# Turning queries one step and keys three steps sooner inside the next half head's projections (differential attention, one core)

## The chip, the cores and the metric

The kernel runs on one core of a Trainium2 chip. The metric is the device time of one execution in microseconds; smaller is better. TensorE (PE in the profile, with its weight loads as PEld) does the matrix products, VectorE (DVE), ScalarE (ACT) and GpSimd (POOL) the element-wise work, and SyncE (SP) issues the DMAs.

## The reference

One decoder layer over 1024 tokens of width 1024: three branches (mLSTM, causal differential attention, cross-attention into a memory of 256 tokens) run on the same normalised input `h`, are gated, merged and projected, and an MLP follows. The change touches the differential attention, with 8 heads, each with two queries and two keys of width 64 and one value of width 128:

```python
def diff_attention(q, k, v, q_g, k_g, lam, subln_g, lam_init):
    q = rms_norm(q, q_g)
    k = rms_norm(k, k_g)
    ...
        s = jnp.einsum('bhcqd,bhckd->bhcqk', qblk, kt).astype(jnp.float32) * scale
        ...
        s = jnp.where(kpos[None, :] <= qpos[:, None], s, -jnp.inf)
        p = jax.nn.softmax(s, axis=-1)
        a = p[:, :, 0] - lam * p[:, :, 1]
        return jnp.einsum('bhqk,bhkv->bhqv', a.astype(vt.dtype), vt)
    ...
    o = rms_norm(o, subln_g) * (1.0 - lam_init)
```

## The kernel before, in words

**Numbers.** A float32 operand is kept as two parts, `hi` and `lo`: `split` (lines 107 to 115) has ScalarE cast the source to `hi` (L111, or L114 with a scale) and VectorE subtract it to get `lo` (L112, or L115). A product `mm3` (line 117) is three matmuls, hi·hi, hi·lo and lo·hi.

**Two streams woven into one.** `branch_d` runs a generator of projections, `d_gemm`, and between its steps issues the attention of the heads already projected. The projections go by half heads, j = 0 to 15: head j // 2, and tokens 0 to 511 (even j) or 512 to 1023 (odd j). A half head has four token tiles i of 128 tokens. A tile is eight steps k; a step is one `mm3`, that is three matmuls of 128x384 which add one slice of the contraction into a PSUM tile of the tag `mm`. So a half head has 32 steps, numbered i * 8 + k. After step 7 of a tile its result is read out of PSUM four times: a copy of query and key to `draw` (L947, ScalarE), their squares to `dscr` (L949, ScalarE), and the split of v into `dv` (L111 on ScalarE, then L112 on VectorE). The sums of squares go to `drr` (L953, VectorE) and, once for the four tiles, through POOL (L127, L128) to the reciprocal norms.

**Two PSUM banks take turns.** `mm_tile` hands out the tags `mm0` and `mm1` in turn, one bank each. While one tile is summed in one bank, the other bank holds the tile before it until that has been read.

**Turning.** The scores need queries and keys with the head's width along the partitions. `prep(raws, rr, vh)` returns three actions for the half head just projected, each with the step of the *next* half head behind which it is issued:

- `q_`: four transposes on TensorE (tile `pr`) of the queries of the four token tiles, put into the bank that is not being summed (`other_tile`, line 96); a split of the result into the tile `dsg` (L114, L115); four DMAs from `dsg` to `dq` (L882, SP's queue).
- `s_`: four multiplications on VectorE that scale the keys in `draw` by their norms (L887).
- `k_`: four transposes of the keys (again `pr`, in `other_tile`), a split into `dsg` (L111, L112), four DMAs from `dsg` to `dk` (L894, SP's queue).

There is one buffer of `dsg`, two of `dq` and four of `dk`. The turned tile stays in its bank until its split is done; the next token tile's projection starts in that same bank.

**The order on each engine.** With `pinned` set, `mm` and `transpose` keep TensorE's instructions in the order in which the program issues them (lines 86 to 94), and the four multiplications of `s_` are pinned among themselves and with these. The other instructions of VectorE, ScalarE, POOL and SP are ordered by a planner when the program is built, within their dependencies.

**Where the steps fall.** Ahead of the attention 60 steps of the projections are issued. Then, for each s (8 per head: a block of 128 queries), `branch_d` issues `scores(s, 0)`, three steps, `values(s-2)`, two steps, `scores(s, 1)`, one step, `turn(s-1, 0)`, one step, `turn(s-1, 1)`, one step and `combine(s)`; the norm of a finished half head is put in at three places. The very first s has seven steps and all others eight, so from then on the steps behind `scores(s, 0)` are k = 3, 4, 5 of a tile, those behind `values(s-2)` are 6 and 7, and 0, 1 and 2 follow around `turn`. `scores` writes two matmuls per 512 keys (tile `sc`), VectorE adds the mask and takes the maximum (L999), forms the exponential's bias (L1003), and ScalarE takes the exponential into `dpe` (L1007). `combine` forms the difference of the two softmaxes on VectorE (L1016, L1017, L1020), `turn` transposes it (tile `tp`) and splits it into `daT`, `values` multiplies it with `dv` (tile `po`, then L1058 on ScalarE and L1059 on VectorE into `doS`), and `norm` squares `doS` (L1068), sums it (L1070), takes the power on POOL (L127, L128), scales `doS` (L1074) and transposes and stores it (L1080, L327).

The last half head's three actions run within the steps of the gates that follow (`for n in range(NK * 4)`), with the same numbers.

Of the kernel before, what the change touches and what calls it, by code (L numbers as in the profile page):

```python
# [31 lines left out]
def f32(ap):  # L32
    return ap.bitcast(F32)
# [38 lines left out]
class Layer:  # L72
# [786 lines left out]
    def d_gemm(self, pool, kv, done):  # L859
# [5 lines left out]
        def prep(raws, rr, vh):  # L865

            qT = pool.tile([P, 2, 512], F32R, tag="dq", name=self.name("dq"))
            kk = pool.tile([P, 2, 2, 512], F32R, tag="dk", name=self.name("dk"))
            rows = [slice(0, 64), slice(64, 128)]

            def turned(j):
                pt = self.other_tile()
                for i in range(4):
                    self.transpose(pt[:, i * P : (i + 1) * P], raws[i][:, j * P : (j + 1) * P])
                return pt, pool.tile([P, 2, 512], F32R, tag="dsg", name=self.name("dsg"))

            def q_():
                pt, sg = turned(0)
                self.split(sg[:, 0], sg[:, 1], pt, self.gd)
                for c in range(2):  # L880
                    for h in range(2):
                        nc.sync.dma_start(f32(qT[rows[h], c]), f32(sg[rows[c], h]))  # L882

            def s_():
                for i in range(4):
                    k_ = raws[i][:, P : 2 * P].rearrange("p (c d) -> p c d", c=2)
                    self.pin(V.tensor_mul(k_, k_, rr[:, i, 2:4].unsqueeze(2).broadcast_to([P, 2, 64])))  # L887

            def k_():
                pt, sg = turned(1)  # L890
                self.split(sg[:, 0], sg[:, 1], pt)
                for c in range(2):
                    for h in range(2):
                        nc.sync.dma_start(f32(kk[rows[h], :, c]), f32(sg[rows[c]]))  # L894
                kv.append((qT, kk[:, 0], kk[:, 1], vh, rr))

            return [(4, q_), (5, s_), (13, k_)]

        raw = {}

# [14 lines left out]
        for j in range(16):  # L915
# [40 lines left out]
            rl = rr.rearrange("p a b -> p (a b)")  # L956
            self.rsqrt_mean(rl, rl, 64, 16)
            late = prep(raws, rr, vh)
            assert j < 4 or done[0] >= (j // 2 - 1) * 8
        for n in range(NK * 4):  # L960
# [810 lines left out]
```

## Time and profile before

| | |
|---|---|
| median of three runs | 2213.79 us (2211.71 to 2217.8) |
| the profiled execution's own time | 2213.57 us |
| its span, first to last instruction | 2211.8 us |
| mean granted clock of TensorE | 0.995 |
| VectorE busy | 1361.4 us (62%) |
| ScalarE busy | 980.7 us (44%) |
| POOL busy | 527.8 us (24%) |

Times within the trace count from the span's start. A timeline row gives start, duration, engine, line, operation, the tile written and the tiles read with their shapes, and the number of instructions merged into it; in brackets stands how long the engine was idle before it, and whose end released it. A row of waits gives the waiting instruction and the one waited for, the total in us, how often, and the longest. PE's ends are modelled and overlap the next start. Letters in tile names are the program's own, without buffer numbers.

### The profile page before, as it was taken

The numbers are of one execution on the slowest core, as the hardware profiler recorded it, in microseconds if no ns is written. First come the engines' busy times: TensorE is split into PE (matmuls) and PEld (weight loads), VectorE is DVE, ScalarE is ACT, GpSimd is POOL, SyncE is SP. The second block draws the span as 40 slices with busy tenths as digits, with TensorE's granted clock in tenths as the row PEclk, the third lists the DMA queues.
The fourth block names the chain that finished last, engine by engine and source line by source line (L and its number), as shares of the span: only waits on it lengthen the run. The fifth ranks groups of instructions, "written<-read, shape, count | busy, mean of one in ns | idle before, by whom it ended". The sixth has DMA issues, their size and how long they took to land.

```text
span 2211.8 us, 30588 instructions
## 1 busy us (share of the span) xinstructions
PE 2163.4 (98%) x11097; PEld 1860.7 (84%) x11097; DVE 1361.4 (62%) x2598; ACT 980.7 (44%) x1962; POOL 527.8 (24%) x696
## 2 busy tenths in 40 slices
PE   7999999999999999999999999999999999899999
PEld 5878888898899999999888888877787888688887
DVE  6643575565237777777641232544688877767779
ACT  6543355454336666666542120223444444543332
POOL 2100000000011111111000003202557655565553
PEclk9999999999999999999999999999999999999999
DMA  7023122121333333333343443436435444854444
GB/s 250 29 81 115 50 91 76 44 82 39 107 109 86 93 84 84 88 92 86 101 148 114 134 142 126 138 110 205 147 115 198 159 147 147 318 196 146 145 145 170
DMA packets 127948, 273.06 MB, mean 123 GB/s; under 512 B 12945, under 2 KB 21430, under 8 KB 125750
## 3 DMA queue, kind: packets, MB, share of 16 engines
q1 hardware_dynamic: 125494, 258.53, 37.2%
q10 hardware_dynamic: 2304, 12.58, 1.4%
q8 instruction: 87, 1.43, 0.3%
q14 instruction: 63, 0.52, 0.1%
HBM read 178.76 MB, written 67.14 MB: 111 GB/s over the span
## 4 chain that ended last, share of the span: by engine, by line
PE 77%; DVE 9%; DMA 6%; ACT 4%; issue 2%; POOL 2%; SPq 0%; DVEq 0%; ACTq 0%; POOLq 0%
PE mm L91 46%; PE p L91 20%; PE sc L91 6%; PE tp L94 2%; PE po L91 2%; DVE acc L67 1%; DMA kraw<-y 1%; DMA xr<-h_d 1%; DVE wo L67 1%; DMA y<-yd 1%; DVE u L67 1%; DVE w L112 1%; DMA wraw<-in_wup 0%; DVE xts L67 0%; DVE c L67 0%
## 5 line engine op out<-in xcount | busy, mean ns | idle before, releaser
L91 PE MATMUL mm<-w,hT 128*128 128x384 f32 (+3 forms) x2496 | 473.4, 332 | 8.3 <-DVE dsg L112 5.4
L91 PE MATMUL mm<-hT,w 128*128 128x512 f32 x1920 | 465.7, 395 | 0.0
L91 PEld LDWEIGHTS mm<-hT,w 128*128 128x128 f32 x1920 | 353.5, 188 | 74.2
L91 PEld LDWEIGHTS mm<-w,hT 128*128 128x128 f32 x2496 | 389.2, 190 | 22.2 <-DVE dsg L112 7.6
L91 PE MATMUL p<-xd,wo 128*128 128x512 f32 x1344 | 310.0, 393 | 5.7 <-DVE c L67 2.2
L91 PE MATMUL p<-xo,wo 128*128 128x512 f32 x1344 | 308.2, 390 | 5.7 <-DVE st L1418 2.6
L91 PEld LDWEIGHTS p<-xd,wo 128*128 128x128 f32 x1344 | 253.8, 189 | 61.7 <-DVE c L67 3.3
L91 PEld LDWEIGHTS p<-xo,wo 128*128 128x128 f32 x1344 | 251.0, 188 | 61.5 <-DVE u L67 3.7
L91 PE MATMUL mm<-kt,w 128*128 128x512 f32 x1152 | 262.2, 389 | 1.9 <-ACT w L111 1.1
L112 DVE TENSOR_TENSOR w<-raw,w 128x256 fp32r<-128x256 f32 (+3 forms) x304 | 173.0, 590 | 137.9 <-ACT w L111 136.8
L91 PEld LDWEIGHTS mm<-kt,w 128*128 128x128 f32 x1152 | 216.0, 188 | 47.9 <-ACT w L111 1.5
L111 ACT CAST w<-raw 128x256 fp32r<-128x256 f32 (+3 forms) x304 | 154.3, 530 | 178.9 <-PE mm L91 114.5
L104 ACT CAST wo<-wraw 128x896 fp32r<-128x896 f32 x122 | 115.0, 945 | 208.9 <-PE p L91 115.2
L67 DVE TENSOR_TENSOR wo<-wraw,wo 128x896 fp32r<-128x896 f32 x122 | 143.7, 1195 | 59.4 <-ACT wo L104 59.4
L1145 POOL TENSOR_TENSOR wraw<-wraw 128x128 f32<-128x128 f32 x128 | 97.3, 760 | 245.8 <-DMA wraw<-in_wdown 108.1
L1007 ACT ACTIVATE dpe<-sc,dst,drr 128x256 f32<-128x256 f32 (+7 forms) x128 | 106.7, 834 | 99.7 <-DVE dst L1003 92.0
L999 DVE CUSTOM_DVE_ANT_0 sc<-sc,tmask 128x256 f32<-128x256 f32 (+7 forms) x128 | 97.0, 758 | 12.6 <-PE sc L91 12.5
L127 POOL TENSOR_SCALAR hss<-hss 128x4 f32<-128x4 f32 x8 | 3.3, 410 | 415.4 <-ACT mscr L752 272.9
L91 PE MATMUL sc<-dk,dq 128*128 128x512 f32 (+3 forms) x384 | 90.4, 343 | 0.0
L1148 POOL TENSOR_TENSOR wraw<-wraw 128x128 f32<-128x128 f32 x128 | 85.6, 669 | 10.0
L1146 POOL TENSOR_TENSOR wraw<-wraw 128x128 f32<-128x128 f32 x128 | 87.3, 682 | 0.0
L1147 POOL TENSOR_TENSOR wraw<-wraw 128x128 f32<-128x128 f32 x128 | 87.2, 682 | 0.0
(283 smaller groups left out, 2832.6 us busy)
## 6 DMA issues: line engine op xcount, KB each, us to landing
dk<-dsg SPq DMA_DIRECT2D x64, 256.0 KB, 4.4
wraw<-in_wup SPq DMA_DIRECT2D x64, 256.0 KB, 3.4
r_d<-xts SPq DMA_DIRECT2D x16, 1024.0 KB, 4.1
wraw<-in_wdown SPq DMA_DIRECT2D x64, 256.0 KB, 3.1
xd<-r_d SPq DMA_DIRECT2D x19, 768.0 KB, 7.4
xd<-r_d SPq DMA_DIRECT2D x14, 1024.0 KB, 6.8
raw<-in_wgate SPq DMA_DIRECT2D x48, 256.0 KB, 3.2
gates<-gt SPq DMA_DIRECT2D x48, 256.0 KB, 2.0
```

The lines of the kernel that those rows point to most:

```text
L67: return self.tc.keep_in_program_order(f(*a, **k))
L91: self.pin(self.nc.tensor.matmul(out, l, r, start=start, stop=stop))
L94: self.pin(self.nc.tensor.transpose(out, x, self.ident))
L104: self.A.copy(hi, src)
L111: nc.scalar.copy(hi, src)
L112: nc.vector.tensor_sub(lo, src, f32(hi))
L999: V.tensor_tensor_reduce(out=sc[:, 0:n], in0=sc[:, 0:n], in1=self.tmask[:, D - n : D], scale=1.0, scalar=-3.0e38, op0=ALU.add, op1=ALU.max ...
L1007: nc.scalar.activation(pe[c][:, 0:n], sc[:, 0:n], AF.Exp, bias=t8[:, 2 + c : 3 + c], scale=rr[:, i, c : c + 1], accum_out=t8[:, 4 + c : 5 ...
L1145: G.tensor_add(r[:, 4], r[:, 0], r[:, 3])
L1146: G.tensor_sub(r[:, 5], r[:, 4], r[:, 1])
L1147: G.tensor_sub(r[:, 6], r[:, 1], r[:, 0])
L1148: G.tensor_sub(r[:, 7], r[:, 2], r[:, 5])
```

## The change

Only the two numbers that say behind which step of the next half head the queries and the keys are turned are changed: the queries go from behind step 4 to behind step 3 of the first token tile, the keys from step 13 to step 10, that is from behind step 5 to behind step 2 of the second tile. The scaling of the keys stays behind step 5 of the first tile.

```diff
@@ -894,7 +894,7 @@
                         nc.sync.dma_start(f32(kk[rows[h], :, c]), f32(sg[rows[c]]))
                 kv.append((qT, kk[:, 0], kk[:, 1], vh, rr))
 
-            return [(4, q_), (5, s_), (13, k_)]
+            return [(3, q_), (5, s_), (10, k_)]
 
         raw = {}
 
```

## The prediction

> **What bounds the kernel now.** I read the page first, then the stretch of differential attention alone (busy time by window), then who waits for whom on TensorE and on its weight loads, and last the timeline of single half heads.
>
> ```profile
> span 2211.8 us, 30588 instructions
> ...
> PE 2163.4 (98%) x11097; PEld 1860.7 (84%) x11097; DVE 1361.4 (62%) x2598; ACT 980.7 (44%) x1962; POOL 527.8 (24%) x696
> ```
> ```profile
> 576.00:1130.00 554.00, 547.94 (x3345) 514.57 (x3344) 378.46 (x1091) 315.48 (x787) 69.42 (x64) 1.00 0.37 94
> ```
>
> TensorE bounds the kernel, and this stretch too: 547.94 of 554.00 us busy, at a granted clock of 1.00. So only TensorE's own waits can be won or lost. On the weight-load queue (PEld), then on the matmuls, they are:
>
> ```profile
> PEld mm L91 <- DVE dsg L112: 7.6, 7, 1.3
> PEld mm L91 <- DVE dsg L115: 0.9, 2, 0.7
> PEld po L91 <- DVE daT L112: 0.4, 1, 0.4
> ```
> ```profile
> PE mm L91 <- DVE dsg L112: 5.4, 7, 0.9
> ```
>
> All but the last end with a half of the split of a turned tile: L112 is that of the keys, L115 that of the queries. The turned tile lies in the PSUM bank that the next token tile's projection needs. The rows of one half head whose keys make TensorE wait:
>
> ```profile
> 776.89 0.63 ACT L1068 ACTIVATE dscr<-doS 128x512 f32<-128x512 f32 x1 [1.16 <-DVE doS L1059]
> ...
> 777.55 0.69 DVE L1070 TENSOR_REDUCE dso<-dscr 128x4 f32<-128x512 f32 x1 [0.30 <-ACT dscr L1068]
> ...
> 778.01 0.36 PEld L91 LDWEIGHTS sc<-dk,dq 128*128 128x128 f32 x2
> ...
> 778.25 0.29 DVE L112 TENSOR_TENSOR dv<-mm,dv 128x128 fp32r<-128x128 f32 x1
> ...
> 779.65 0.69 DVE L1074 TENSOR_TENSOR doS<-doS,dso 128x512 f32<-128x512 f32 x1 [0.51 <-POOL dso L128]
> ...
> 780.10 0.60 PE L94 MATMUL pr<-ident,draw 128*128 128x128 f32 x4
> ...
> 781.05 0.48 DVE L1020 SCALAR_TENSOR_TENSOR dpe<-dpe,dst,dpe 128x256 f32<-128x256 f32 x1
> 781.22 0.67 ACT L1007 ACTIVATE dpe<-sc,dst,drr 128x384 f32<-128x384 f32 x1 [1.54 <-DVE dst L1003]
> ...
> 781.89 0.57 ACT L111 CAST dsg<-pr 128x512 fp32r<-128x512 f32 x1
> ...
> 782.50 0.69 DVE L112 TENSOR_TENSOR dsg<-pr,dsg 128x512 fp32r<-128x512 f32 x1 [0.96 <-ACT dsg L111]
> ...
> 783.24 0.47 PEld L91 LDWEIGHTS mm<-w,hT 128*128 128x128 f32 x3 [1.23 <-DVE dsg L112]
> 783.24 0.79 PE L91 MATMUL mm<-w,hT 128*128 128x384 f32 x3 [0.92 <-DVE dsg L112]
> ...
> 783.87 0.38 PE L94 MATMUL tp<-ident,dpe 128*128 128x128 f32 x2
> ```
>
> The key transposes (pr) end at 780.70, but ScalarE casts them only at 781.89: the exponential (L1007) stands ahead of the cast in its queue, and waits for VectorE, which has been held up behind POOL (L1074, 0.51). The subtraction ends at 783.19, and 0.05 us later the next tile's loads start. Such a wait comes once per head, when the second half's keys are turned. ACT and VectorE do not follow the program's order: L1074 is the second part of a norm, written two scores steps behind its first part (L1070), yet runs 2.1 us after it. The planner orders what is not pinned; TensorE's order is fixed.
>
> **The keys, three steps sooner.** Nothing is added or removed: four transposes (0.60), the cast (0.57), the subtraction (0.69) and four DMAs move. On TensorE they pass out of the group after scores(s+1, 0) and land ahead of those scores, behind step 2 of the second tile; here that is the place of the load at 778.01, 2.1 us ahead of 780.10. Transposes from 778.6 to 779.2, then the cast and the subtraction without the exponential of 781.22 ahead of them, free the bank at about 780.5 (779.2 + 0.57 + 0.69), or at 781.2 with one more operation of 0.69 ahead on VectorE. The next tile wants it at about 782.0 (783.24 less 1.23). So the seven key waits should go: 7.6 us. A wait gives some back: three loads take 0.47 us right after it and 0.54 elsewhere (1012.10, below), 0.07 each. 7.6 - 7 x 0.07 = **7.1 us won**.
>
> The weight-load row is taken rather than the matmul's 5.4, because the load itself waited: it started with its matmul at 783.24. [...]
>
> **What is late next.** The sooner transposes overwrite the bank of the first tile, whose last reader is the subtraction of v (L112 dv). Here it ends at 778.54, so a load can start at 778.59 instead of 778.01: 0.58 late, less 0.07, 0.51 lost. Behind it waits everything on TensorE. The first and the last of the five half heads of this kind (58.4 us apart), the next one, and one of the other kind:
>
> ```profile
> 719.59 0.36 PEld L91 LDWEIGHTS sc<-dk,dq 128*128 128x128 f32 x2
> ...
> 719.83 0.29 DVE L112 TENSOR_TENSOR dv<-mm,dv 128x128 fp32r<-128x128 f32 x1
> ```
> ```profile
> 953.29 0.36 PEld L91 LDWEIGHTS sc<-dk,dq 128*128 128x128 f32 x2
> ...
> 953.56 0.29 DVE L112 TENSOR_TENSOR dv<-mm,dv 128x128 fp32r<-128x128 f32 x1
> ```
> ```profile
> 1011.54 0.29 DVE L112 TENSOR_TENSOR dv<-mm,dv 128x128 fp32r<-128x128 f32 x1
> ...
> 1011.75 0.36 PEld L91 LDWEIGHTS sc<-dk,dq 128*128 128x128 f32 x2
> ...
> 1012.10 0.54 PEld L91 LDWEIGHTS mm<-w,hT 128*128 128x128 f32 x3
> ```
> ```profile
> 746.32 0.28 DVE L112 TENSOR_TENSOR dv<-mm,dv 128x128 fp32r<-128x128 f32 x1
> ...
> 747.10 0.82 PEld L91 LDWEIGHTS sc<-dk,dq 128*128 128x128 f32 x4
> ```
>
> The same step gives 0.58 at 719.59, 0.61 at 953.29, 0.13 at 1011.75 and nothing at 747.10, where the bank is free 0.45 us ahead. Five times 0.51 and 0.06: **2.6 us lost**. Its bounds are nothing (the dv split comes sooner) and the whole gain (the wait merely moves); I take the rows.
>
> The cast and the subtraction now run ahead of the combine (L1020) and the scores' chain. That costs VectorE 0.69 ahead of the combine, which ends at 781.53 for transposes at 783.87: 2.34 of slack less 0.69 and less the 1.2 by which TensorE comes sooner. It holds, by 0.4 us.
>
> **The queries, one step sooner.** A step is three matmuls, 0.52 us (six from 771.35 to 772.39 below). Their place among the attention steps stays, since steps 3 to 5 are one group.
>
> ```profile
> 771.35 1.21 PE L91 MATMUL mm<-w,hT 128*128 128x384 f32 x6
> ...
> 771.80 1.28 DVE L112 TENSOR_TENSOR daT<-tp,daT 128x512 fp32r<-128x512 f32 x2
> ...
> 772.39 0.60 PE L94 MATMUL pr<-ident,draw 128*128 128x128 f32 x4
> ...
> 773.19 1.98 PEld L91 LDWEIGHTS po<-dv,daT 128*128 128x128 f32 x16
> ...
> 773.77 0.56 ACT L1007 ACTIVATE dpe<-sc,dst,drr 128x256 f32<-128x256 f32 x1 [1.76 <-DVE dst L1003]
> ...
> 774.33 0.68 ACT L114 ACTIVATE dsg<-pr,dv 128x512 fp32r<-128x512 f32 x1
> ...
> 775.03 2.41 SPq L882 DMA_DIRECT2D dq<-dsg  x4
> 775.04 0.75 DVE L115 SCALAR_TENSOR_TENSOR dsg<-pr,dv,dsg 128x512 fp32r<-128x512 f32 x1 [1.36 <-ACT dsg L114]
> ```
> ```profile
> DMA to landing us min/median/max: 2.2/2.3/2.6
> ```
>
> Here ScalarE takes the queries at 774.33, behind an exponential that waited for VectorE, so 0.52 us sooner transposes change nothing; the wait of 0.7 with L115 is of this kind and stays. The other, 0.2, is covered by 0.52 and goes. Their four DMAs (2.41 of SP's time, landed 2.3 after issue, so near 779.2) read the only dsg buffer, which the keys' cast wants at 779.2: no wait, or one inside the slack above. The key DMAs pass no other transfer in SP's queue here.
>
> Sum: -7.1 - 0.2 + 2.6 = **-4.7 us**. The profiled execution took 2213.57 us around its span of 2211.8; -4.7 gives 2208.9. The median of the three runs is 0.22 higher, hence 2209.1. Everything behind the stretch hangs on TensorE's end and moves along.
>
> **Rivals.** *Queries flip.* If the planner puts the query cast ahead of the exponential, it runs in ScalarE's 1.76 us of idle time, from about 772.5 instead of 774.33. VectorE's query subtraction and what waits behind it (the scaling of the keys, L1059, through it L1068 at 776.89, the first tile's reads and the dv split) may then come up to 1.8 us sooner; 0.6 is enough for the dv split to end ahead of 778.01, and both L115 waits go as well. Then 7.6 + 0.9 - 9 x 0.07 = 7.9 us are won: 2213.79 - 7.9 = 2205.9. For it speak the 0.52 us of lead, against it today's order in just these half heads.
>
> *No change in ScalarE's queue.* The key cast stays behind the exponential. TensorE would lose 0.58 at the transposes, but the chain that ends at 783.19 runs over POOL, VectorE and ScalarE, so the later wait shrinks by as much: 2213.8, the change not doing what it says. Against it: the turned keys are ready 2 us ahead of that exponential.
>
> *Slower: query split ahead of the attention split.* VectorE splits two daT tiles (771.80, 1.28) just ahead of the values' loads at 773.19. Were the query subtraction (L115, 0.75) set ahead of the second one, it would wait for its cast (772.5 + 0.68), end near 773.95 and daT near 774.6: 1.4 us late, in seven heads 10 us. With the -4.7 that is 2219. It decides as soon as these two change places; against it, the second daT is ready first, by about 1 us.
>
> **How the numbers follow.** Forecast 0.50, queries flip 0.30, no change 0.10, slower 0.06, the rest 0.04 for orders that shift elsewhere. The range runs from under the flip to over no change: 2205.0 to 2214.5; the ends leave under a microsecond each for scatter between runs. About 0.3% (6.6 us, under 2207.2 or over 2220.4) can be told from no change: the flip gives most of "faster" (0.24 of its 0.30, and 0.05 of the forecast), the slower rival, which lies just inside that bound, and the rest give 0.06 together, and 0.65 is left for "same".
>
> **What would show it.** Waits of loads on DVE dsg L112 fall from 7.6 to under 1 us, and new ones of pr on DVE dv L112 appear, five of 0.5 to 0.6; the cast of the keys stands ahead of the exponential; heads come 57.8 us apart instead of 58.4. I am wrong if mm still waits for dsg L112 by more than 2 us, if pr waits in more than seven half heads, or if po begins to wait for daT.

## The result and the profile after

| | before | after |
|---|---|---|
| median | 2214.02 us (16 runs, 2211.55 to 2218.55) | 2208.58 us (16 runs, 2203.87 to 2211.56) |
| ratio after / before | | 0.9973, 95% interval 0.9965 to 0.9981 |
| the profiled execution's own time, its span | 2213.57, 2211.8 us | 2207.4, 2205.3 us |

By the interval the change is 4.2 to 7.7 us faster. The forecast was 2209.1, so the number was met; the mechanism behind it was not the forecast's but that of the first rival, *queries flip*. The page and the stretch of differential attention (busy time by window), after:

```profile
span 2205.3 us, 30616 instructions
...
PE 2162.5 (98%) x11097; PEld 1862.0 (84%) x11097; DVE 1360.7 (62%) x2598; ACT 982.2 (45%) x1962; POOL 525.2 (24%) x696
```
```profile
576.00:1130.00 554.00, 553.47 (x3387) 521.90 (x3386) 380.41 (x1095) 319.14 (x791) 70.55 (x66) 1.00 0.37 97
```

TensorE's work is as before (2162.5 us against 2163.4), and of these 554 us it now idles 0.53 instead of 6.06. What is left of its waits in this window, on the weight loads and then on the matmuls:

```profile
PEld po L91 <- DVE daT L112: 0.9, 2, 0.5
PEld pr L94 <- DVE dv L112: 0.2, 1, 0.2
```
```profile
PE po L91 <- DVE daT L112: 0.5, 2, 0.3
```

No row names dsg any more: the 7.6 us of key waits and the 0.9 of query waits are gone, and the new wait of the transposes (pr) for the bank's last reader (dv), forecast at 2.6 us, came once with 0.2. The two waits of po are not new. Before the change there were two as well, but the later one (1132.75 us) lies behind the end of the window that the prediction read. From 1060 to 1140 us the loads' waits before are:

```profile
PEld po L91 <- DVE daT L112: 0.9, 2, 0.5
```

The stage can be measured by the 64 copies of query and key out of PSUM: first and last start, before and then after:

```profile
L947 ACT COPY draw<-mm x64: 353/373/381, 624.2 to 1059.9; 128x256 f32<-128x256 f32 x64
```
```profile
L947 ACT COPY draw<-mm x64: 353/372/376, 624.3 to 1052.2; 128x256 f32<-128x256 f32 x64
```

That is 435.7 us before and 427.9 after: 7.8 us won in this stage. The po waits lie behind it in both. The same half head as in the prediction, after the change (timeline):

```profile
769.27 1.28 DVE L112 TENSOR_TENSOR daT<-tp,daT 128x512 fp32r<-128x512 f32 x2
769.32 0.60 PE L94 MATMUL pr<-ident,draw 128*128 128x128 f32 x4
...
769.96 0.69 ACT L114 ACTIVATE dsg<-pr,dv 128x512 fp32r<-128x512 f32 x1 [0.48 <-PE pr L94]
...
771.19 0.75 DVE L115 SCALAR_TENSOR_TENSOR dsg<-pr,dv,dsg 128x512 fp32r<-128x512 f32 x1
771.24 0.56 ACT L1007 ACTIVATE dpe<-sc,dst,drr 128x256 f32<-128x256 f32 x1 [0.59 <-DVE dst L1003]
...
773.61 0.63 ACT L1068 ACTIVATE dscr<-doS 128x512 f32<-128x512 f32 x1 [0.42 <-DVE doS L1059]
...
775.09 0.28 DVE L112 TENSOR_TENSOR dv<-mm,dv 128x128 fp32r<-128x128 f32 x1
...
775.49 0.51 PEld L94 LDWEIGHTS pr<-ident,draw 128*128 128x128 f32 x4
775.64 0.60 PE L94 MATMUL pr<-ident,draw 128*128 128x128 f32 x4
...
776.41 0.57 ACT L111 CAST dsg<-pr 128x512 fp32r<-128x512 f32 x1
...
777.73 0.68 DVE L112 TENSOR_TENSOR dsg<-pr,dsg 128x512 fp32r<-128x512 f32 x1
```

Read it against the rows of before. There the exponential (L1007, 773.77) ran ahead of the query cast (L114, 774.33). Now the cast stands first, waits 0.48 us for the query transposes, and the exponential follows. Measured from the start of the query transposes, the cast starts 0.64 us later where it was 1.94, and the last read of the first tile (dv) ends 6.05 us later (775.37 less 769.32) where it was 6.15. Since these transposes are themselves issued one step (0.52 us) sooner, that read comes 0.6 us sooner in TensorE's order, just what the bank was short of by the prediction's rows (0.58): the key transposes' loads start at 775.49, with no wait. The key cast comes at 776.41 with no exponential of the next scores ahead of it, and the bank is free at 778.41, over a microsecond before the next tile starts in it (its loads start at 779.45).

### The profile page after: what moved, and what is told of

The parts are those of the page before. It is cut to its first block, busy times and chain, and to the rows that moved or that the text cites. A ratio compares the mean times of both kernels' runs of the same rounds, so it can differ in the third digit from the quotient of the medians.

```text
span 2205.3 us, 30616 instructions
## 1 busy us (share of the span) xinstructions
PE 2162.5 (98%) x11097; PEld 1862.0 (84%) x11097; DVE 1360.7 (62%) x2598; ACT 982.2 (45%) x1962; POOL 525.2 (24%) x696
## 4 chain that ended last, share of the span: by engine, by line
PE 86%; DVE 5%; DMA 4%; ACT 2%; issue 2%; POOL 1%; SPq 0%; DVEq 0%; ACTq 0%; POOLq 0%
PE mm L91 51%; PE p L91 22%; PE sc L91 6%; PE po L91 3%; PE tp L94 3%; DVE acc L67 1%; PE pr L94 1%; DVE wo L67 1%; DVE u L67 0%; DVE w L112 0%; DMA kraw<-y 0%; PE tp L91 0%; DMA wraw<-in_wdown 0%; DVE xts L67 0%; DMA xr<-h_d 0%
## 5 line engine op out<-in xcount | busy, mean ns | idle before, releaser
L112 DVE TENSOR_TENSOR w<-raw,w 128x256 fp32r<-128x256 f32 (+3 forms) x304 | 172.8, 588 | 138.2 <-ACT w L111 137.1
L1007 ACT ACTIVATE dpe<-sc,dst,drr 128x256 f32<-128x256 f32 (+7 forms) x128 | 106.7, 833 | 95.5 <-DVE dst L1003 92.1
```

The costliest lines, as they stand in the source:

```text
L112: nc.vector.tensor_sub(lo, src, f32(hi))
L1007: nc.scalar.activation(pe[c][:, 0:n], sc[:, 0:n], AF.Exp, bias=t8[:, 2 + c : 3 + c], scale=rr[:, i, c : c + 1], accum_out=t8[:, 4 + c : 5 ...
```

## The experiments

Two theories. **F**: the keys' sooner place takes the key waits away, but by itself would put a wait for the bank's last reader in their place; what takes that one away is the exchange on ScalarE (the query cast ahead of the exponential), which comes with the query step. **K**: the keys' place alone does everything. In the table "stage" is the distance from the first to the last of the 64 copies, "loads waited" the sum of the waits of TensorE's weight loads between these two copies, and the ratio is against before on the same chip. The rows of waits under the single experiments take in the whole attention (from 576 us to 1130, or to 1140 in the last three), so they hold a few waits more, those of po among them.

| kernel | queries, keys behind step | stage, us | less than before | loads waited, us | median, us | ratio (95%) |
|---|---|---|---|---|---|---|
| before | 4, 13 | 435.7 | | 8.5 | 2213.95 / 2216.04 | |
| after | 3, 10 | 427.9 | 7.8 | 0.2 | 2208.58 | 0.9973 (0.9965 to 0.9981) |
| q_only | 3, 13 | 432.4 | 3.3 | 4.9 | 2210.22 | 0.9979 (0.9971 to 0.9988) |
| k_only | 4, 10 | 431.7 | 4.0 | 4.7 | 2208.87 | 0.9977 (0.9968 to 0.9987) |
| no_exchange | 3, 10, ScalarE as before | 431.4 | 4.3 | 4.3 | 2210.05 | 0.9979 (0.9969 to 0.9988) |
| after_again | 3, 10 | 427.9 | 7.8 | 0.2 | 2206.61 | 0.9967 (0.9954 to 0.9980) |
| keys_9 | 3, 9 | 431.3 | 4.4 | 4.6 | 2210.73 | 0.9979 (0.9970 to 0.9989) |
| keys_11 | 3, 11 | 428.0 | 7.7 | 0.0 | 2209.07 | 0.9968 (0.9956 to 0.9980) |
| later | 5, 14 | 446.4 | -10.7 | 19.1 | 2228.41 | 1.0048 (1.0032 to 1.0064) |

The medians of before are those beside the first four experiments and beside the last three, which ran on another chip. The intervals of the ratios overlap for all but the last; what tells the kernels apart is the stage and the waits. Each stage comes from one profile, that of the full change from two, which agree. Turned into times the ratios say 4.6 to 7.3 us less than before for the first seven kernels and 10.6 more for the last, each within 2 us of its stage.

**q_only**: the query step alone.

```diff
-            return [(4, q_), (5, s_), (13, k_)]
+            return [(3, q_), (5, s_), (13, k_)]
```

> Queries one step sooner, keys as before. Theory F (the exchange): in the half heads whose keys made TensorE wait, ScalarE takes the query cast (L114) ahead of the exponential (L1007), VectorE's chain behind it runs about 0.5 us sooner, so the key waits (DVE dsg L112) shrink from 7.6 us in total to about 4 to 5, and both query waits (DVE dsg L115, 0.9) go: 3 to 4 us faster than before, some 4 us slower than the full change. Rival K (the keys' place alone): the query step does nothing but take away the 0.2 us wait; key waits stay at 7.6 and the time within 0.5 us of before.

The waits of its weight loads:

```profile
PEld mm L91 <- DVE dsg L112: 5.1, 8, 0.7
PEld po L91 <- DVE daT L112: 0.4, 1, 0.4
```

and the two instructions of ScalarE in question, with the key cast, in the timeline:

```profile
772.88 0.69 ACT L114 ACTIVATE dsg<-pr,dv 128x512 fp32r<-128x512 f32 x1 [0.49 <-PE pr L94]
...
774.15 0.57 ACT L1007 ACTIVATE dpe<-sc,dst,drr 128x256 f32<-128x256 f32 x1 [0.58 <-DVE dst L1003]
...
781.74 0.58 ACT L111 CAST dsg<-pr 128x512 fp32r<-128x512 f32 x1
```

Theory F's numbers: the query step alone exchanges cast and exponential, the query waits go, the longest key wait falls from 1.3 to 0.7 us, and 3.3 us of stage are won. The key waits come to 5.1 us (4.9 in the stage), just at the upper end of what was expected. Theory K expected next to nothing.

**k_only**: the key steps alone.

```diff
-            return [(4, q_), (5, s_), (13, k_)]
+            return [(4, q_), (5, s_), (10, k_)]
```

> Keys three steps sooner, queries as before. Theory F: the query cast stays behind the exponential, so the sooner key transposes come ahead of the last read of their bank (DVE dv L112): key waits on DVE dsg L112 under 1 us, new waits of the pr loads on DVE dv L112 in five half heads, 0.5 to 0.6 us each (2.6 in all), the waits on DVE dsg L115 unchanged at 0.9: 4 to 5 us faster than before, some 3 us slower than the full change. Rival K: no new waits, the whole 7 us of the stage come from the keys alone and the time is that of the full change within 1 us.

The waits of the loads:

```profile
PEld pr L94 <- issue: 3.6, 6, 0.7
PEld mm L91 <- DVE dsg L115: 0.9, 2, 0.7
PEld po L91 <- DVE daT L112: 0.9, 2, 0.5
PEld mm L91 <- DVE dsg L112: 0.2, 1, 0.2
```

and one of the new waits in the timeline, with ScalarE in the order of before:

```profile
773.06 0.57 ACT L1007 ACTIVATE dpe<-sc,dst,drr 128x256 f32<-128x256 f32 x1 [1.76 <-DVE dst L1003]
...
773.62 0.68 ACT L114 ACTIVATE dsg<-pr,dv 128x512 fp32r<-128x512 f32 x1
...
777.55 0.29 DVE L112 TENSOR_TENSOR dv<-mm,dv 128x128 fp32r<-128x128 f32 x1
...
777.96 0.42 PEld L94 LDWEIGHTS pr<-ident,draw 128*128 128x128 f32 x4 [0.68 <-issue]
777.99 0.63 PE L94 MATMUL pr<-ident,draw 128*128 128x128 f32 x4 [0.38 <-DVE dv L112]
```

The loads' row names no releaser ("issue"); the matmul's row, at the same place, names dv. Here ScalarE's order is the one that the forecast assumed, and what the forecast described is there: hardly a key wait (0.2), the wait of 0.7 for L115, and new waits ahead of pr. These are larger than expected: six, 3.6 us in all, five of them 0.7 long, where 2.6 us was expected. The stage is 4.0 us better than before, against 4.5 by the forecast without its 0.2 for the queries. The median alone would not refute theory K: 2208.87 is within 0.3 us of the full change's 2208.58 and 2.3 above its second measurement. The six waits and the stage do, 3.8 us longer than with the full change.

**no_exchange**: the full change with ScalarE's order of before. The exponential of scores(s, 0) and the query cast are kept in program order in the half heads concerned; on every engine the instructions then stand as in the full change, but for this exchange and a few rows of VectorE and ScalarE near the start of the attention.

```diff
@@ in q_(), for odd j
-                self.split(sg[:, 0], sg[:, 1], pt, self.gd)
+                self.pin(nc.scalar.activation(sg[:, 0], pt, AF.Copy, scale=self.gd))
+                V.scalar_tensor_tensor(
+                    out=sg[:, 1], in0=pt, scalar=self.gd, in1=f32(sg[:, 0]), op0=ALU.mult, op1=ALU.subtract
+                )
@@ in scores(), the exponential
-            nc.scalar.activation(
+            ex = nc.scalar.activation(
...
+            if c == 0 and s % 8 == 1:
+                self.pin(ex)
```

> The full change with one thing undone: in the half heads with odd number the exponential of scores(s, 0) and the query cast are kept in program order on ScalarE, as before the change; all else is as in the full change. Theory F: the pr loads wait again for DVE dv L112 in five half heads by 0.5 to 0.6 us, one query wait of 0.7 on DVE dsg L115 comes back, none on DVE dsg L112 for the keys: the stage is 3.2 us longer than with the full change, 4.7 us shorter than before. Rival K: waits and times are those of the full change within 0.5 us in the stage.

```profile
PEld pr L94 <- issue: 3.5, 6, 0.7
PEld mm L91 <- DVE dsg L881: 0.6, 1, 0.6
PEld po L91 <- DVE daT L112: 0.4, 1, 0.4
PEld pr L94 <- DVE dv L112: 0.2, 1, 0.2
```

In these rows of the loads' waits (L881 is the query subtraction in this kernel) the pr waits are back, and the query wait too. In the timeline of the same half head the exponential (L1013 here) stands ahead of the query cast (L880 here) again, and the last read of the first tile ends 6.69 us behind the start of the query transposes (780.78 less 774.09), against 6.05 in the full change:

```profile
774.09 0.60 PE L94 MATMUL pr<-ident,draw 128*128 128x128 f32 x4
...
776.00 0.56 ACT L1013 ACTIVATE dpe<-sc,dst,drr 128x256 f32<-128x256 f32 x1 [1.76 <-DVE dst L1009]
...
776.56 0.68 ACT L880 ACTIVATE dsg<-pr,dv 128x512 fp32r<-128x512 f32 x1
...
780.49 0.29 DVE L112 TENSOR_TENSOR dv<-mm,dv 128x128 fp32r<-128x128 f32 x1
```

With 431.4 us the stage is 3.5 longer than in the full change, where 3.2 was expected, and 4.3 shorter than before, where 4.7 was. The two kernels differ in hardly more than which of two ScalarE instructions runs first, in seven half heads, so the exchange is shown to be worth these 3.5 us. Against k_only (431.7) this kernel has the query step without the exchange: that is worth 0.3 us.

**after_again**: the full change once more, unaltered.

> The full change itself, once more. Theory S (scatter): the attention stage again ends 7.5 to 8 us sooner than in the profile of before, and what the rest of the kernel adds or takes differs from profile to profile by up to 3 us either way. Rival G (given back): the rest again gives back about 1.5 to 2.5 us, so the span is 5.5 to 6.5 us shorter than that of before although the stage ends 7.8 us sooner.

The stage is 427.9 us again, and the span is 8.1 us shorter than that of before. The rest of the span (span less stage) was 1776.1 us in the profile of before, 1777.4 in that of after and 1775.8 here, so it gives nothing back by rule: theory S. It lies between 1774.9 (k_only) and 1780.0 (no_exchange) in the profiles of the first four experiments, and between 1780.1 and 1783.0 in the last three, on the other chip. This scatter is nearly as large as the effect, which is why one span or one median does not show the stage's 7.8 us cleanly. The mean granted clock was 0.996 in the profile of k_only and 0.993 in that of later; in those of before and after it was 0.995, with 1.00 from 576 to 1130 us and 0.99 behind that, so a part of the scatter may be the clock's; the runs do not separate it.

**keys_9** and **keys_11**: the keys one step sooner still, and one step less, with the queries behind step 3.

```diff
-            return [(3, q_), (5, s_), (10, k_)]
+            return [(3, q_), (5, s_), (9, k_)]
```
```diff
-            return [(3, q_), (5, s_), (10, k_)]
+            return [(3, q_), (5, s_), (11, k_)]
```

> Queries behind step 3 as in the full change, keys one step sooner still, behind step 9 (step 1 of the second tile). In the profile of the full change the pr loads of the half heads with odd number start only about 0.05 us after the last read of their bank (DVE dv L112) allows it. Theory F (what is late next is the bank): a step is 0.52 us, so in seven of these half heads pr waits about 0.45 us for DVE dv L112, 2.5 to 3.5 us in all; none in the others, which have some 0.75 us in hand. The stage is about 3 us longer than with the full change, 5 us shorter than before. Rival S (sooner is always better or free): no wait, stage as with the full change within 0.3 us.

> Queries behind step 3 as in the full change, keys behind step 11, two steps sooner than before instead of three. The planner puts the key cast ahead of the exponential here too. Theory F (the place in ScalarE's queue decides, not the number of steps): no waits for DVE dsg L112 and none of pr for DVE dv L112; the stage is as long as with the full change within 0.3 us. Rival S (each step sooner gives its share): the waits for DVE dsg L112 keep a third of 7.6 us, and the stage is 2 to 3 us longer than with the full change.

The loads' waits of keys_9, then of keys_11:

```profile
PEld pr L94 <- issue: 3.8, 7, 0.5
PEld po L91 <- DVE daT L112: 0.9, 2, 0.5
PEld pr L94 <- DVE dv L112: 0.8, 2, 0.7
PEld pr L94 <- ACT gt L471: 0.3, 1, 0.3
```
```profile
PEld po L91 <- DVE daT L112: 0.9, 2, 0.5
```

One step sooner, the pr loads wait in the seven half heads expected, about 0.54 us each, and in two more (0.8 us together) that were expected to have time in hand; the stage is 3.4 us longer than in the full change. One step later nothing is lost: 428.0 us. So a step has no worth of its own. The keys' place must lie behind the last read of the bank and early enough for their cast to stand ahead of the exponential; steps 10 and 11 do both, step 13 (q_only) is too late, and 12 was not run. keys_11 leaves more in hand: its timeline has the subtraction of v and the loads of pr 0.97 us apart (775.27 + 0.28, 776.52), the full change 0.12, and the key cast still stands ahead of the next exponential.

```profile
775.27 0.28 DVE L112 TENSOR_TENSOR dv<-mm,dv 128x128 fp32r<-128x128 f32 x1
...
776.52 0.53 PEld L94 LDWEIGHTS pr<-ident,draw 128*128 128x128 f32 x4
...
777.38 0.59 ACT L111 CAST dsg<-pr 128x512 fp32r<-128x512 f32 x1 [0.68 <-ACT dpe L1007]
...
778.34 0.67 ACT L1007 ACTIVATE dpe<-sc,dst,drr 128x384 f32<-128x384 f32 x1 [0.38 <-DVE dst L1003]
```

**later**: queries and keys one step later than before.

```diff
-            return [(4, q_), (5, s_), (13, k_)]
+            return [(5, q_), (5, s_), (14, k_)]
```

> The other way: queries behind step 5, keys behind step 14, each one step later than before. Theory F: each key wait grows by a step (0.52 us) and by the copy of the values' output (L1058, 0.37 us), which now stands ahead of the key cast on ScalarE, and the half heads with even number, so far just without a wait, get one of 0.3 to 0.9 us: 6 to 14 us slower than before, all of it in the stage, as waits for DVE dsg L112. Rival: the waits were filled from elsewhere (POOL and VectorE hold the chain), so the time moves by less than 2 us.

```profile
PEld mm L91 <- DVE dsg L112: 16.5, 16, 1.6
PEld mm L91 <- DVE dsg L115: 2.2, 4, 0.8
PEld tp L94 <- DVE doS L1059: 1.1, 5, 0.2
PEld po L91 <- DVE daT L112: 0.4, 1, 0.4
```

Its loads wait for the keys in all 16 half heads, and the stage is 10.7 us longer, where 6 to 14 was expected. The waits are not filled from elsewhere: a microsecond of them is about a microsecond of stage (10.6 us more of the loads' waits, 10.7 of stage). One part of the expectation failed. The key waits that were 1.2 us before were to grow by the step (0.52) and by L1058 (0.37); they are 1.6 and have grown by the second alone. In these half heads the cast stands behind the exponential and L1058, so that the transposes' later place adds nothing:

```profile
787.59 0.67 ACT L1007 ACTIVATE dpe<-sc,dst,drr 128x384 f32<-128x384 f32 x1 [1.55 <-DVE dst L1003]
...
788.25 0.35 ACT L1058 ACTIVATE doS<-po,dst 128x128 f32<-128x128 f32 x1
788.50 0.58 ACT L111 CAST dsg<-pr 128x512 fp32r<-128x512 f32 x1
```

Nor is all of it waits for DVE dsg L112: of the 10.6 us by which the loads wait longer in the stage, the query waits (L115) have 1.3 and those of tp 1.1.

## Why the prediction was right, and where it was wrong

- **TensorE's waits are what can be won**: right. Its work stayed, and the stage became 7.8 us shorter where the loads' waits in it fell by 8.3 (8.5 to 0.2). The 0.07 us that the prediction takes off for each of the nine waits gone, 0.6 in all, is about the difference.
- **The keys, 7.1 us won**: right in its mechanism. No dsg L112 wait is left in the full change, 0.2 us in k_only. The reason given, a cast that no longer stands behind the exponential of the next scores, is in the rows at 776.41, and its counterpart at 781.74 in q_only, where the keys are late. The bank came free 2.8 us behind the start of the transposes (778.41 less 775.64), where the text had 1.9, or 2.6 with one more operation ahead on VectorE; the next tile left room for that.
- **What is late next, 2.6 us lost**: right for the kernel that was imagined, wrong for this one. With ScalarE's order of before (k_only, no_exchange) the waits came, at the half heads named and with 0.4 us by the matmuls and 0.7 by the loads against 0.58 expected. In the full change none of these is left; its only pr wait, 0.2 us, is that of the very first half head.
- **The queries: "so 0.52 us sooner transposes change nothing"**: this is the step that failed. It took ScalarE's order for given in a place of which the text itself said that the planner orders it. With the 0.52 us the planner put the cast first, in the idle time that the row [1.76 <-DVE dst L1003] showed; why its choice turns on them is not shown. This was the rival *queries flip*, given 0.30. The sum gave the query step 0.2 us; with the keys moved it is worth 3.8 (k_only to after), 0.3 of it the step without the exchange and 3.5 the exchange. The rival's price, 7.9 us, is what the stage shows (7.8).
- **The sum and the time**: that 2209.1 was so near 2208.58 is luck: the sum's -4.7 is not what the stage did (-7.8), and what lies outside the stage made up the difference. The stage alone would give 2213.79 - 7.8 = 2206.0. The median of 16 runs lies 2.6 above that, and 7.8 is just beyond the upper end of the interval (4.2 to 7.7); after_again's 2206.61 lies at it. That the scatter outside the stage makes this difference fits the profiles but is not shown for the unprofiled runs.
- **The distance of heads**: 57.8 us was forecast, and the key transposes of the same half head in the next head start 57.3 us later (775.64 and 832.92), which fits the rival: 58.4 less the whole key wait of a head, 1.2, with nothing given back at pr.
- **No change in ScalarE's queue** did not happen, nor did **slower**: the second daT split still runs ahead of the query subtraction (769.27 and 771.19), and po waits as often and as long as before (twice, 0.9 us). Of the three signs of being wrong none came, so they did not tell the forecast from the flip; the absent pr waits did.

## What to carry to other kernels

Where a planner orders an engine's queue, a small move on another engine can exchange two instructions there, and the exchange can be worth nearly as much as the move itself (here 3.5 us, beside the 4.0 of the keys' move alone): look for idle time ahead of an instruction that waits, with ready work behind it. A transposed tile that borrows a bank in a pair has a window, from the last read of that bank to the start of the next tile less the split's time. As early as it will go is not the best place in it: here one step too early cost 3.4 us of stage, and one step later than the change has it cost 0.1 and left more in hand.

## What the runs showed that was not expected

A wait of TensorE has two prices in these profiles, and the weight load's, which the prediction took, holds over a wider range than it needed. From before to later the loads' waits in the stage rose by 10.6 us (8.5 to 19.1) and the stage by 10.7, while the matmuls' idle time rose by 6.4 only (5.9 to 12.3). From before to after the loads' waits fell by 8.3 and the matmuls' idle time by 5.9, and the stage by 7.8. In all the kernels the loads' waits give the stage's change within 0.8 us.

The loads did not run ahead into the waits looked at: load and matmul start together (783.24 before), or 0.03 us apart (777.96 and 777.99 in k_only), where loads without a wait of their own started 0.17 us ahead of their matmul (779.45 and 779.62 after) or less (778.12 and 778.17).
